# First MLP product by one Strassen step with seven half-k products in place of eight, interleaved with the second product

## The chip, the cores and the metric

The kernel runs on one core of one Trainium2 chip. The metric is the device time of one execution in microseconds (us), from the first to the last instruction with what the launch adds around them; lower is better. The engines are named as in the profile: PE is TensorE's matmul stream, PEld its weight loads, DVE is VectorE, ACT ScalarE, POOL GpSimd, and SP is SyncE, which issues nearly all DMAs, in order.

## The reference

One layer with two token groups (128 prompt tokens, 512 latent tokens; 640 rows together) and shared weights. The change touches the last line but two only:

```python
def layer(x, mod, p, lru_h0, gla_s0, rows):
    sh1, sc1, g1, sh2, sc2, g2 = jnp.split(mod, N_MOD, axis=-1)
    ng = p['norm_g']
    h = rmsnorm(x, ng[0]) * (1.0 + sc1) + sh1
    m, s_lru, s_gla = token_mix(h, p, lru_h0, gla_s0, rows)   # two recurrent mixers, w_out
    x = x + g1 * rmsnorm(m, ng[1])
    h = rmsnorm(x, ng[2]) * (1.0 + sc2) + sh2
    f = jnp.square(jax.nn.relu(h @ p['mlp_w1'])) @ p['mlp_w2']   # 640x1024 by 1024x4096, 640x4096 by 4096x1024
    x = x + g2 * rmsnorm(f, ng[3])
    return x, s_lru, s_gla
```

## The kernel before

Every fp32 product is made of three fp32r products: each operand x is split into a rounded part hi and a rest lo (ACT casts hi, DVE subtracts lo; `split_act` for activations, `split_piece` for weights), and PE adds hi*hi, hi*lo and lo*hi in PSUM.

The kernel records its whole program as a list of operations through `Recorder`, and `Recorder.order` then sets the order on each engine: a list scheduler with a cost for each operation, which gives out the buffers of each pool, respects data dependencies (`add` finds them by memory region), and prefers the operation recorded first (weight splits count as recorded 50 places earlier, `SPLIT_AHEAD`). Before the change, `region` treats a whole PSUM tile of two banks as one region. So a change of any dependency can move instructions anywhere in the program.

The MLP is cut into 16 groups g of 256 hidden columns (two blocks f of 128). In a group, `w1_units` makes hidden block f with features on partitions: 8 k-blocks by 3 terms by two halves of 320 rows, so 96 matmuls of 320 columns for the two blocks; `post_ff` takes relu (ACT), square (DVE), and the hi and lo parts `ah`, `al`. `w2_units` then multiplies with 256 rows of `mlp_w2`: 5 row tiles t by 2 blocks by 3 terms by 2 spans of 512 columns, 60 matmuls; `post_f` adds the result to the accumulators `fa`, `fb` in SBUF (DVE). In the main loop the units stand as w1 of group g, then w2 of group g-1. The first two groups (`NHALF` = 2) are made in two parts (rows 0 to 383, then the rest), because the rows of tiles 3 and 4 come later from the output projection (`out_pass`, `post_out`, `post_out_T`); `post_out_T` transposes the normed rows and writes the hi and lo parts H2H and H2L of the MLP's input. The last two groups of w2 share one pass with the final norm, gate and store (`post_f` with g = 15).

What the change leans on: the pool `tp` holds 43 tiles of 128 x 662 (`t_`), `wp` 4 split weight pieces (hi and lo each), `rawp` 2 raw weight loads of 1 MB, PSUM two `dense` and two `aux` tiles of two banks. The residual rows after the first half of the layer (`x1`, names xra and xrb in the trace) stay in ten tiles of `tp` until the end. A chain of DVE work that makes the gate rows g2 (`mod_chain`, names mw, mac) is fed in from group `G2_FROM` = 2 on. All operations are issued in one line of a helper, L340 in the profile, so groups are told apart by tile names.

```python
    for g in range(NHALF, NG):
        w1_units(g)
        if g == G2_FROM:
            units[-1].before = lambda: chains.extend(mod_g2)
        if g < NG - 1:
            w2_units([g - 1])
```

Of the kernel before, what the change touches and what calls it, by code (L numbers as in the profile page):

```python
# [8 lines left out]
F32 = mybir.dt.float32  # L9
F32R = mybir.dt.float32r  # L10
# [5 lines left out]
KT = 8  # L16
# [21 lines left out]
MH_ENG = "VAVV"  # L38
SPLIT_AHEAD = 50
POOL_OUT = (5,)  # L40
G2_FROM = 2
N_WARM = 24


# [65 lines left out]
class Recorder:  # L110
# [54 lines left out]
    @staticmethod  # L165
    def region(ap):

        return (0, 128, ((0, 1 << 30),)) if ap.space == bass.MemoryType.PSUM else _region(ap)

    def add(self, eng, name, args, kw):  # L170
        out = kw["out"] if "out" in kw else args[0]
        writes = [out] + ([kw["accum_out"]] if "accum_out" in kw else [])
        reads = [a for a in list(args if "out" in kw else args[1:]) + [v for k, v in kw.items() if k not in ("out", "accum_out")]
                 if hasattr(a, "ap")]
        if name == "copy_predicated" or (name == "matmul" and not kw["start"]):
            reads.append(out)
        o = Op()
        o.eng, o.name, o.args, o.kw, o.idx = eng, name, args, kw, len(self.ops)
        o.us = self.cost(eng, name, args, kw, out)
        o.rank = (o.idx - self.ahead, o.idx)  # L180
        o.users, o.tiles, o.ready, o.done, o.at = [], [], 0.0, None, None
        o.table = self.TABLE.get(args[2]) if name == "activation" else None
        deps = {}
        acc = [(a, True) for a in writes] + [(a, False) for a in reads]
        for a, w in acc:
            nm = getattr(a.tensor, "name", None)
            if a.space not in (bass.MemoryType.SB, bass.MemoryType.PSUM):
                continue
            r = self.region(a)
            if nm in self.tile_of and nm not in o.tiles:  # L190
                o.tiles.append(nm)
            h = self.hist.setdefault(nm, [])
            for q, qw, qr in h:
                both = a.space == bass.MemoryType.PSUM and q.eng != eng
                if (w or qw or both) and q is not o and _meet(r, qr):
                    deps[q.idx] = q
        for a, w in acc:
            if a.space not in (bass.MemoryType.SB, bass.MemoryType.PSUM):
# [144 lines left out]
class Piece:  # L343


    def __init__(self, load, view, rep=None):
        self.load, self.view, self.rep = load, view, rep
        self.hi = self.lo = None
        self.pool = False


# [37 lines left out]
def tile_hybrid_layer(  # L389
# [30 lines left out]
    def aux():  # L420
        return rec.tile(psa, 2, [128, 2, 512], F32, "aux", "a")
# [157 lines left out]
    def split_piece(p):  # L579
        hi = rec.tile(wp, N_W, [128, 1024], F32R, "whi", "whi")  # L580
        src = p.view(p.load.raw)
        lo = None
        if p.rep:
            hv = hi.rearrange("p (a r b) -> p a r b", a=KT, r=p.rep)
            for r in range(p.rep - 1):
                A.copy(hv[:, :, r, :], src)
            V.tensor_tensor(hv[:, :, p.rep - 1, :], src, f32(hv[:, :, 0, :]), op=OP.subtract)
        else:
            lo = rec.tile(wp, N_W, [128, 1024], F32R, "wlo", "wlo")
            hv = hi.rearrange("p (a b) -> p a b", a=src.shape[1])  # L590
            lv = lo.rearrange("p (a b) -> p a b", a=src.shape[1])
            A.copy(hv, src)
            (G if p.pool else V).tensor_tensor(lv, src, f32(hv), op=OP.subtract)
        p.hi, p.lo = hi, lo
        p.load.left -= 1
# [581 lines left out]
            after=lambda: prev is None or prev.done))  # L1177


    grow = {}  # L1180

    def mod_chain(part, nm, j, name):

# [41 lines left out]
        def fin_rows():  # L1225
            gi = 1 if nm == "g1" else 3
            br, gr = t_("br"), t_("gr")
            SP.dma_start(out=br[:, 0:512], in_=b_mod[0:1, col0:col0 + 512].to_broadcast([128, 512]))
            SP.dma_start(out=gr[:, 0:512], in_=norm_g[0, gi:gi + 1, 512 * j:512 * (j + 1)].to_broadcast([128, 512]))
            ps = aux()  # L1230
            for i in range(2):
                hi, lo = t_("mach", F32R), t_("macl", F32R)
                split_act(s["acc"][i][:, 0:512], hi[:, 0:512], lo[:, 0:512])
                for x in (hi, lo):
                    PE.matmul(ps[:, i, :], ones, x[:, 0:512], start=x is hi, stop=x is lo)
            for i in range(2):
                t = grow[nm, i, j] = t_(nm)
                V.tensor_tensor(t[:, 0:512], ps[:, i, :], br[:, 0:512], op=OP.add)
                V.tensor_tensor(t[:, 0:512], t[:, 0:512], gr[:, 0:512], op=OP.mult)

        fin = Stage(fin_rows if nm in ("g1", "g2") else fin_cols, 2.4 if nm in ("g1", "g2") else 0.4, gap=2)
        prev = mod_list[-1] if mod_list else None
# [124 lines left out]
        SP.dma_start(out=b[:, 0:512], in_=src[..., 512:1024])  # L1367
        xr[t] = (a, b)

    nrms = {}  # L1370

    def post_out(t, ps):
        i = 0 if t == 0 else 1
# [21 lines left out]
            nrm.append(n_)  # L1395
        nrms[t] = nrm

    def post_out_T(t):
        i, nrm = 0 if t == 0 else 1, nrms[t]
        ts = slice(128 * t, 128 * (t + 1))  # L1400
        for j in range(2):
            pst, hx = aux(), t_("hx")
            for k in range(4):
                PE.transpose(pst[:, 0, 128 * k:128 * (k + 1)], nrm[j][:, 128 * k:128 * (k + 1)], ident)
            for c0 in range(4):
                k = 4 * j + c0
                dst, src = hx[:, 128 * c0:128 * (c0 + 1)], pst[:, 0, 128 * c0:128 * (c0 + 1)]
                if j:
                    act(dst, src, AF.Identity, scale=cols["a2"][:, i, k:k + 1], bias=cols["sh2"][:, i, k:k + 1])
                else:  # L1410
                    V.tensor_scalar(dst, src, cols["a2"][:, i, k:k + 1], cols["sh2"][:, i, k:k + 1],
                                    op0=OP.mult, op1=OP.add)
            hv = hx[:, 0:512].rearrange("p (k c) -> p k c", k=4)
            split_act(hv, hbox["h"][:, 4 * j:4 * j + 4, ts], hbox["l"][:, 4 * j:4 * j + 4, ts])

    def out_pass(tiles, kinds):
        st = {}
# [3 lines left out]
        for u in range(4):  # L1421
            def run(t, u=u):
# [77 lines left out]
    NG = DFF // 256  # L1500

    HALVES, THIRDS = ((0, 512), (512, 1024)), ((0, 512), (512, 768), (768, 1024))

# [27 lines left out]

    def w2_units(gs):

        pcs = [row_pieces(mlp_w2, 2 * g) for g in gs]
        for t in range(NT):
            st = {}

# [7 lines left out]
            def run(n, t=t, st=st):  # L1545
# [3 lines left out]
                if n == 0:  # L1549
                    if last:  # L1550
                        st["ps"] = [p[:, 0, 0:c1 - c0] for p, (c0, c1) in zip((dense(), aux(), dense()), spans)]
                    else:
                        ps = dense() if t % 2 == 0 else aux()
                        st["ps"] = [ps[:, j, :] for j in range(2)]
                pss = st["ps"]
                if last:
# [10 lines left out]
                    post_f(t, pss, gs[-1], spans)  # L1567

            for n in range(len(gs)):
                units.append(Unit(pcs[n], [lambda n=n, run=run: run(n)], lambda: None, f"w2_{gs[n]}_{t}", us=2.6))  # L1570

    NHALF = 2
    n_mlp = len(units)
    for g in range(NHALF):
        w1_units(g, 0, 384, pair=g == 0)
# [3 lines left out]
    def before_rest():  # L1579
        for t in range(3, NT):  # L1580
            post_out_T(t)

    units[n_mlp + 2].before = before_rest
    for g in range(NHALF - 1):
        w2_units([g])
    for g in range(NHALF, NG):
        w1_units(g)
        if g == G2_FROM:
            units[-1].before = lambda: chains.extend(mod_g2)
        if g < NG - 1:  # L1590
            w2_units([g - 1])
    n_last = len(units)
    w2_units([NG - 2, NG - 1])
    units[n_last].before = lambda: flush(mod_g2)


    pieces, loads = [], []
# [83 lines left out]
```

## Time and profile before

| what | us |
|---|---|
| median of 3 runs | 1164.29 (1162.61 to 1165.95) |
| the profiled execution's own time | 1160.65 |
| its span (first to last instruction) | 1158.9 |
| PE busy in it | 1131.3 |
| PEld busy | 1064.3 |
| DVE busy | 755.6 |
| ACT busy | 557.8 |

The profile is of one execution. Busy time of an engine is the time in which it has an instruction in work; a wait is put down to the event that ended it. PE's rows give a start and a modelled length, and lengths of neighbours overlap, so the pace of matmuls is read from their starts.

### The profile page before, as it was taken

To read this page: it belongs to the slowest core of one execution; us is meant where nothing else is said; L and a number is where in the kernel's file an instruction comes from. 1 tells how busy PE (TensorE), PEld (TensorE's weight loads), DVE (VectorE), ACT (ScalarE), POOL (GpSimd) and SP (SyncE) were. 2 spreads that over 40 slices of the span, in tenths; PEclk is the share of its full clock that TensorE was granted. 3 is DMA by queue.
4 is the path that set the end of the run, shared out by engine and by line. 5 is a ranking of instruction groups with operands and counts; after the bars stand their busy time and mean duration, and the time that the engine had idled before them with its cause. 6 is when DMAs were issued, how large, how long until landed. Compare 5 with 4: busy or idle time off the path is not lost.

```text
span 1158.9 us, 17719 instructions
## 1 busy us (share of the span) xinstructions
PE 1131.3 (98%) x7188; PEld 1064.3 (92%) x7188; DVE 755.6 (65%) x1147; ACT 557.8 (48%) x882; POOL 80.1 (7%) x152
## 2 busy tenths in 40 slices
PE   6999999999999999999999999999999999999996
PEld 5899899999999999999999879999999989999995
DVE  4687885966557557549968389885444555555546
ACT  6387989994657668213432388422222222222222
POOL 3135112000000000000000021000000000000001
PEclk9999999999999999999999999999999999999999
DMA  9835445332121312245535356532222222222202
GB/s 296 253 78 142 132 110 132 93 104 77 52 92 40 102 60 83 64 158 207 191 128 182 112 179 199 192 118 74 73 73 74 73 73 73 78 81 86 85 1 90
DMA packets 101009, 130.63 MB, mean 113 GB/s; under 512 B 7790, under 2 KB 77632, under 8 KB 100928
## 3 DMA queue, kind: packets, MB, share of 16 engines
q1 hardware_dynamic: 98880, 127.61, 35.6%
q0 software_dynamic: 2048, 1.90, 0.7%
q8 instruction: 56, 0.92, 0.3%
q14 instruction: 25, 0.20, 0.1%
HBM read 117.94 MB, written 3.68 MB: 105 GB/s over the span
## 4 chain that ended last, share of the span: by engine, by line
PE 78%; DVE 8%; ACT 5%; DMA 5%; issue 2%; POOL 1%; SPq 0%; DVEq 0%; POOLq 0%; ACTq 0%
PE dense L340 62%; PE aux L340 16%; DVE i L340 2%; DVE th L340 2%; DMA i<-r 1%; DVE wlo L340 1%; DMA modw<-in_w_mod_dram 1%; ACT L340 1%; ACT r L340 1%; ACT th L340 1%; DMA raw<-in_w_in_dram 1%; DMA w2raw<-in_gla_w_dram 1%; DMA r<-r 1%; ACT whi L340 1%; ACT L339 0%
## 5 line engine op out<-in xcount | busy, mean ns | idle before, releaser
L340 ACT CAST whi<-raw 128x1024 fp32r<-128x1024 f32 (+1 forms) x159 | 164.5, 1038 | 394.2 <-PE dense L340 363.6
L340 DVE TENSOR_TENSOR wlo<-raw,whi 128x1024 fp32r<-128x1024 f32 x154 | 188.1, 1223 | 173.5 <-ACT whi L340 173.1
L340 PE MATMUL dense<-HH,whi 128*128 128x320 f32 x768 | 178.1, 312 | 0.2 <-ACT vc L340 0.2
L340 PE MATMUL dense<-HL,whi 128*128 128x320 f32 x768 | 176.1, 310 | 0.0
L340 PE MATMUL dense<-HH,wlo 128*128 128x320 f32 x752 | 172.4, 309 | 0.0
L340 PEld LDWEIGHTS dense<-HH,whi 128*128 128x128 f32 x768 | 128.4, 188 | 2.1 <-issue 0.8
L340 PEld LDWEIGHTS dense<-HL,whi 128*128 128x128 f32 x768 | 128.9, 188 | 0.0
L340 PEld LDWEIGHTS dense<-HH,wlo 128*128 128x128 f32 x752 | 125.9, 188 | 0.0
L340 PE MATMUL dense<-H2H,whi 128*128 128x320 f32 (+2 forms) x496 | 116.8, 309 | 0.0
L340 PE MATMUL dense<-H2H,wlo 128*128 128x320 f32 (+2 forms) x496 | 116.4, 308 | 0.0
L340 PE MATMUL dense<-H2L,whi 128*128 128x320 f32 (+2 forms) x496 | 116.4, 308 | 0.0
L340 PEld LDWEIGHTS dense<-H2H,whi 128*128 128x128 f32 x496 | 84.5, 188 | 1.3
L340 PEld LDWEIGHTS dense<-H2L,whi 128*128 128x128 f32 x496 | 84.0, 188 | 0.0
L340 PEld LDWEIGHTS dense<-H2H,wlo 128*128 128x128 f32 x496 | 84.0, 188 | 0.0
L340 DVE SCALAR_TENSOR_TENSOR mac<-mw,cst,mac 128x512 f32<-128x512 f32 x112 | 77.9, 747 | 2.9 <-DMA mw<-in_w_mod_dram 2.7
L340 PE MATMUL dense<-wlo,ah 128*128 128x512 f32 (+1 forms) x192 | 75.3, 392 | 0.0
L340 PE MATMUL dense<-whi,ah 128*128 128x512 f32 (+1 forms) x192 | 75.3, 392 | 0.0
L340 PE MATMUL dense<-whi,al 128*128 128x512 f32 (+1 forms) x192 | 75.3, 392 | 0.0
L340 PE MATMUL aux<-wlo,ah 128*128 128x512 f32 (+1 forms) x132 | 51.7, 392 | 0.0
L340 PE MATMUL aux<-whi,ah 128*128 128x512 f32 (+1 forms) x132 | 51.7, 391 | 0.0
L340 PE MATMUL aux<-whi,al 128*128 128x512 f32 (+1 forms) x132 | 51.6, 391 | 0.0
L340 PE MATMUL dense<-whi,HH 128*128 128x256 f32 x160 | 45.0, 281 | 0.0
(311 smaller groups left out, 2172.6 us busy)
## 6 DMA issues: line engine op xcount, KB each, us to landing
raw<-in_mlp_w_dram SPq DMA_DIRECT2D x34, 1024.0 KB, 5.7
raw<-in_w_in_dram SPq DMA_DIRECT2D x24, 1024.0 KB, 5.5
mw<-in_w_mod_dram SPq DMA_DIRECT2D x64, 256.0 KB, 5.6
modw<-in_w_mod_dram SPq DMA_DIRECT2D x32, 256.0 KB, 6.1
raw<-in_w_out_dram SPq DMA_DIRECT2D x8, 1024.0 KB, 4.9
i<-r SPq DMA_DIRECT2D x32, 160.0 KB, 2.6
raw<-in_w_in_dram SPq DMA_DIRECT2D x8, 512.0 KB, 4.0
raw<-in_lru_up_dram SPq DMA_DIRECT2D x4, 1024.0 KB, 5.1
```

The costliest lines, as they stand in the source:

```text
L340: getattr(eng[o.eng], o.name)(*o.args, **o.kw)
```

## The change

For groups 2 to 15 the first product is made from a 2 by 2 by 2 split: the 1024 input features are cut into halves of 4 k-blocks, the 640 rows into halves L and R of 320, and the 256 hidden columns of the group are the two blocks. Seven products of half-k (4 k-blocks by 3 terms, 12 matmuls of 320 columns) replace eight. The sums of the inputs are made once (`make_forms`: tiles f42, f42l, f3, and H2H/H2L columns R of features 0 to 511 overwritten), the sums of the weights for each group (`make1` to `make4`, tiles s1, s2, in halves of a weight piece), and the partial results are combined by accumulation in three PSUM banks X, Y, Z of `aux` tiles with copies of the state in between taken by ACT (`sq`) and DVE (`sq`, `z1`, `z2`). The square moves from DVE to ACT (`post`). The four w1 units of a group alternate with the five w2 units of the group before; all w2 tiles of the middle groups use `dense` banks.

Around it: `region` now knows PSUM by bank; `post_out_T` keeps the transposed input in fp32 (hx0 to hx7) and `split_h` splits it in two calls; `post_out` stores the residual rows in DRAM, and `before_last` loads them again ahead of the last two groups of w2; the gate rows g2 go to DRAM and back too; `G2_FROM` is 6.

```diff
-G2_FROM = 2
+G2_FROM = 6
...
-        return (0, 128, ((0, 1 << 30),)) if ap.space == bass.MemoryType.PSUM else _region(ap)
+        if ap.space == bass.MemoryType.PSUM:
+            runs = _region(ap)[2]
+            return (0, 128, ((runs[0][0] // 512 * 512, -(-runs[-1][1] // 512) * 512),))
+        return _region(ap) if ap.space == bass.MemoryType.SB else (0, 128, ((0, 1 << 30),))
...
+        xd[t] = rec.tile(dr, 1, [128, 1024], F32, f"xd{t}", f"xd{t}")
+        for j in range(2):
+            SP.dma_start(out=xd[t][:, 512 * j:512 * (j + 1)], in_=x1[t][j][:, 0:512])
...
-            hv = hx[:, 0:512].rearrange("p (k c) -> p k c", k=4)
-            split_act(hv, hbox["h"][:, 4 * j:4 * j + 4, ts], hbox["l"][:, 4 * j:4 * j + 4, ts])
+
+    def split_h(c0, c1):
+        for k in range(KT):
+            split_act(h32[k][:, c0:c1], hbox["h"][:, k, c0:c1], hbox["l"][:, k, c0:c1])
...
+                    if t == 2:
+                        split_h(0, 384)
...
+    def make_forms(k):
...
+        u, l = h32[k], h32[k + 4]
+        V.tensor_tensor(u[:, L_], u[:, L_], u[:, R_], op=OP.subtract)
+        V.tensor_tensor(u[:, R_], l[:, R_], u[:, R_], op=OP.subtract)
+        V.tensor_tensor(l[:, R_], l[:, R_], u[:, L_], op=OP.add)
+        V.tensor_tensor(l[:, L_], l[:, L_], l[:, R_], op=OP.subtract)
+        split_act(l[:, 0:T], f42[k][:, 0:T], f42l[k][:, 0:T])
+        split_act(u[:, L_], hbox["h"][:, k, R_], hbox["l"][:, k, R_])
+        c = slice(320 * (k % 2), 320 * (k % 2 + 1))
+        split_act(u[:, R_], *(f3[k // 2 * 2 + n][:, c] for n in range(2)))
...
+        def make1(r, hi, lo):
+            s1, s2 = s["s1"], s["s2"] = kv(t_("s1")), kv(t_("s2"))
+            split_act(blk(r, 0, 0), kv(hi), kv(lo))
+            V.tensor_tensor(s1, blk(r, 1, 0), blk(r, 1, 1), op=OP.add)
+            V.tensor_tensor(s2, s1, blk(r, 0, 0), op=OP.subtract)
+            split_act(s2, kv(hi, 1), kv(lo, 1))
...
+        def post(f, z, parts):
+            ah, al = ffs[f] = (t_("ah", F32R), t_("al", F32R))
+            for c in parts:
+                act(z[:, c], z[:, c], AF.Relu)
+            act(z[:, 0:T], z[:, 0:T], AF.Square)
+            split_act(z[:, 0:T], ah[:, 0:T], al[:, 0:T])
...
+        def p1():
+            ps = aux()
+            s["X"], s["Y"], s["q"] = ps[:, 0, L_], ps[:, 1, L_], t_("sq")
+            product(s["X"], 0, 0, "B11", True, False)
+            A.copy(s["q"][:, L_], s["X"])
+
+        def p6():
+            product(s["Y"], 1, 0, "T2", True, False)
+            V.tensor_tensor(s["q"][:, R_], s["q"][:, L_], s["Y"], op=OP.add)
+
+        def p5():
+            s["Z"] = aux()[:, 0, L_]
+            product(s["Z"], 0, 1, "T1", True, False)
+
+        def p7():
+            z = s["z2"] = t_("z2")
+            product(s["Y"], 1, 1, "T3", False, False)
+            V.tensor_tensor(z[:, R_], s["q"][:, L_], s["Y"], op=OP.add)
+            V.tensor_tensor(z[:, R_], z[:, R_], s["Z"], op=OP.subtract)
+
+        def p2():
+            z = s["z1"] = t_("z1")
+            product(s["X"], 0, 2, "B21", False, True)
+            act(z[:, L_], s["X"], AF.Relu)
+
+        def p4():
+            z = s["z2"]
+            product(s["Y"], 1, 2, "T4", False, True)
+            V.tensor_tensor(z[:, L_], s["q"][:, L_], s["Y"], op=OP.add)
+            post(2 * g + 1, z, (slice(0, T),))
+
+        def p3():
+            z = s["z1"]
+            product(s["Z"], 0, 3, "B22", False, True)
+            V.tensor_tensor(z[:, R_], s["q"][:, R_], s["Z"], op=OP.subtract)
+            post(2 * g, z, (R_,))
...
+    for k in range(4):
+        units[n_forms + k].before = lambda k=k: make_forms(k)
     for g in range(NHALF, NG):
-        w1_units(g)
+        a_ = fast_units(g)
...
+        b_ = w2_units([g - 1]) if g < NG - 1 else []
+        for n in range(max(len(a_), len(b_))):
+            units.extend(a_[n:n + 1] + b_[n:n + 1])
...
+        for t in range(NT):
+            x1[t] = (t_("xra"), t_("xrb"))
+            for j in range(2):
+                SP.dma_start(out=x1[t][j][:, 0:512], in_=xd[t][:, 512 * j:512 * (j + 1)])
```

The order that the scheduler makes of it, at three places. First DVE in a middle group, before the change: from the last two adds of one w2 pass over the first product of the next group (wlo are weight splits, rl and al the square and the rest of a hidden block, fa and fb the accumulators).

```order
L340 TENSOR_TENSOR wlo<-raw,whi 128x1024
L340 TENSOR_TENSOR fa<-fa,dense 128x512
L340 TENSOR_TENSOR fb<-fb,dense 128x512
L340 TENSOR_TENSOR wlo<-raw,whi 128x1024 x2
L340 TENSOR_TENSOR rl<-rl 128x640
L340 TENSOR_TENSOR al<-rl,ah 128x640
L340 TENSOR_TENSOR wlo<-raw,whi 128x1024
L340 TENSOR_TENSOR rl<-rl 128x640
```

And DVE in a middle group of the change, from the last fb of one w2 pass over products 6 and 7 of the next group (s are sums of weight blocks, sq and z the partial results).

```order
L346 TENSOR_TENSOR fb<-fb,dense 128x512
L346 TENSOR_TENSOR sq<-sq,aux 128x320
L346 TENSOR_TENSOR wlo<-raw,whi 128x1024
L346 TENSOR_TENSOR fa<-fa,dense 128x512
L346 TENSOR_TENSOR fb<-fb,dense 128x512
L346 TENSOR_TENSOR s_1262<-raw 128x512
L346 TENSOR_TENSOR s_1263<-s_1262,raw 128x512
L346 TENSOR_TENSOR raw<-raw 128x4x128
L346 TENSOR_TENSOR z_1251<-sq,aux 128x320
L346 TENSOR_TENSOR wlo<-s_1233,whi 128x512
L346 TENSOR_TENSOR z_1251<-z_1251,aux 128x320
```

Reads of partial sums (sq, z) now stand between the adds of the second product and the weight sums, one piece of work of DVE after the other.

Second, DVE at the step from the first two groups to group 2: before, with the first w2 pass (fb copies) stood the g2 chain (mac).

```order
L340 COPY fb_1152<-aux_1150 128x512
L340 SCALAR_TENSOR_TENSOR mac_1170<-mw_1180,cst32_113,mac_1170 128x512
L340 SCALAR_TENSOR_TENSOR mac_1171<-mw_1180,cst32_113,mac_1171 128x512
L340 SCALAR_TENSOR_TENSOR mac_1170<-mw_1181,cst32_113,mac_1170 128x512
L340 COPY fb_1155<-dense_1153 128x512
```

In the change the sums of the inputs stand there (hx; f42l and H2L are their rests; whi_1182 and whi_1185 are the next weight pieces, which take the buffers of the two pieces of this w2 pass).

```order
L346 COPY fb_1171<-dense_1169 128x512
L346 TENSOR_TENSOR hx3_1034<-hx3_1034 128x320
L346 TENSOR_TENSOR wlo_1183<-raw_1145,whi_1182 128x1024
L346 TENSOR_TENSOR f42l_1166<-hx6_1037,f42_1165 128x640
L346 TENSOR_TENSOR hx3_1034<-hx7_1038,hx3_1034 128x320
L346 TENSOR_TENSOR wlo_1186<-s1_1148,whi_1185 128x512
L346 TENSOR_TENSOR hx7_1038<-hx7_1038,hx3_1034 128x320
L346 TENSOR_TENSOR raw_1136<-raw_1136 128x4x128
L346 TENSOR_TENSOR hx7_1038<-hx7_1038 128x320
L346 TENSOR_TENSOR H2L_1024<-hx3_1034,H2H_1023 128x320
L346 TENSOR_TENSOR wlo_1186<-raw_1136,whi_1185 128x512
L346 TENSOR_TENSOR f3_1168<-hx3_1034,f3_1167 128x320
```

The next row there is f42l_1173, the last input sum's rest, and then fb_1176<-aux_1174; the first is read by the last three matmuls of group 2's product 6, the second frees the bank of its product 5.

Third, SP near the end of the change, where xd and gd are the rows kept in DRAM and raw the last load of w2's weights.

```order
L346 DMA raw<-in_mlp_w_dram 128x2x1024
L346 DMA g_1632<-gd_1389 128x512
L346 DMA g_1633<-gd_1496 128x512
L346 DMA g_1634<-gd_1391 128x512
L346 DMA g_1635<-gd_1498 128x512
L346 DMA xra<-xd_1030 128x512
L346 DMA xrb<-xd_1030 128x512
L346 DMA xra<-xd_1051 128x512
L346 DMA xrb<-xd_1051 128x512
L346 DMA xra<-xd_1059 128x512
L346 DMA xrb<-xd_1059 128x512
L346 DMA raw<-in_mlp_w_dram 128x2x1024
```

Ten reloads have come in ahead of the last weight load, which before followed the load ahead of it at once.

## Rows read from the trace of the kernel before

**Rows 1.** The page: span, then busy time, share and instructions of engines.

```profile
span 1158.9 us, 17719 instructions
...
PE 1131.3 (98%) x7188; PEld 1064.3 (92%) x7188; DVE 755.6 (65%) x1147; ACT 557.8 (48%) x882; POOL 80.1 (7%) x152
```

**Rows 2.** Windows of stretches: length, busy time of PE, PEld, DVE, ACT, POOL, clock.

```profile
core 0: us, PE busy (x) PEld busy (x) DVE busy (x) ACT busy (x) POOL busy (x), PEclk, DMA share, GB/s
...
100.00:200.00 100.00, 97.11 (x699) 96.23 (x698) 72.26 (x100) 93.39 (x114) 18.69 (x32) 1.00 0.45 122
200.00:300.00 100.00, 97.42 (x699) 95.91 (x698) 74.24 (x114) 74.00 (x104) 1.21 (x1) 1.00 0.33 94
...
660.00:700.00 40.00, 38.24 (x179) 30.82 (x178) 32.31 (x57) 30.65 (x56) 8.20 (x8) 1.00 0.52 155
700.00:740.00 40.00, 40.00 (x251) 37.51 (x250) 37.93 (x67) 25.08 (x51) 2.74 (x3) 1.00 0.72 234
740.00:1120.00 380.00, 380.00 (x2127) 344.47 (x2126) 209.22 (x271) 96.17 (x114) 0.00 (x0) 1.00 0.24 77
...
1150.00:1159.00 9.00, 0.00 (x0) 0.00 (x0) 3.59 (x8) 1.00 (x4) 1.44 (x2) 0.70 0.39 117
```

**Rows 3.** Timeline of PE, one group: start, length, instruction.

```profile
799.50 0.46 PE L340 MATMUL dense<-H2H,whi 128*128 128x320 f32 x2
...
813.59 0.39 PE L340 MATMUL dense<-whi,ah 128*128 128x512 f32 x1
...
827.50 0.45 PE L340 MATMUL dense<-H2H,whi 128*128 128x320 f32 x2
```

**Rows 4.** Timeline of PE, 256-column matmuls, three apart.

```profile
719.73 0.28 PE L340 MATMUL dense<-H2H,wlo 128*128 128x256 f32 x1
...
720.08 0.28 PE L340 MATMUL dense<-H2H,wlo 128*128 128x256 f32 x1
```

**Rows 5.** Groups by shape, 700 to 1130 us: busy, mean ns, idle before.

```profile
L340 PEld LDWEIGHTS dense<-H2H,whi 128*128 128x128 f32 x496 | 84.5, 188 | 1.3
...
L340 DVE TENSOR_TENSOR wlo<-raw,whi 128x1024 fp32r<-128x1024 f32 x66 | 80.7, 1224 | 114.8 <-ACT whi L340 114.6
...
L340 ACT CAST whi<-raw 128x1024 fp32r<-128x1024 f32 x64 | 67.3, 1051 | 244.9 <-PE dense L340 238.4 <-issue 4.6 <-DMA raw<-in_mlp_w_dram 1.8
...
L340 DVE TENSOR_TENSOR fa<-fa,dense 128x512 f32<-128x512 f32 x40 | 27.4, 685 | 19.7 <-PE dense L340 19.7
...
L340 DVE TENSOR_TENSOR al<-rl,ah 128x640 fp32r<-128x640 f32 x28 | 23.0, 822 | 11.3 <-ACT ah L340 11.3
...
L340 ACT CAST ah<-rl 128x640 fp32r<-128x640 f32 x28 | 20.4, 728 | 39.4 <-DVE rl L340 39.4
L340 DVE SCALAR_TENSOR_TENSOR mac<-mw,cst,mac 128x512 f32<-128x512 f32 x28 | 20.3, 747 | 2.9 <-DMA mw<-in_w_mod_dram 2.7
...
L340 DVE TENSOR_TENSOR rl<-rl 128x384 f32<-128x384 f32 x4 | 2.1, 552 | 0.0
...
L340 DVE TENSOR_TENSOR rl<-rl 128x256 f32<-128x256 f32 x4 | 1.7, 424 | 0.6 <-ACT rl L340 0.6
```

**Rows 6.** Timeline: last matmul into a bank, and the add that reads it.

```profile
787.19 0.39 PE L340 MATMUL dense<-whi,al 128*128 128x512 f32 x1
...
787.62 0.69 DVE L340 TENSOR_TENSOR fa<-fa,dense 128x512 f32<-128x512 f32 x1
```

**Rows 7.** Timeline: DVE in the first w2 pass; PE at its end.

```profile
734.65 2.07 DVE L340 SCALAR_TENSOR_TENSOR mac<-mw,cst,mac 128x512 f32<-128x512 f32 x3
...
741.57 0.46 PE L340 MATMUL dense<-H2H,whi 128*128 128x320 f32 x2
```

**Rows 8.** DMA issues: count, KB of one, median us from issue to landing.

```profile
raw<-in_mlp_w_dram SPq DMA_DIRECT2D x34, 1024.0 KB, 5.7
...
mw<-in_w_mod_dram SPq DMA_DIRECT2D x64, 256.0 KB, 5.6
```

More of the change, by code (lines that the diff above doesn't have):

```diff
@@ L186, in add @@
             nm = getattr(a.tensor, "name", None)
-            if a.space not in (bass.MemoryType.SB, bass.MemoryType.PSUM):
+            if not self.tracked(a):
                 continue
@@ L197, in add @@
         for a, w in acc:
-            if a.space not in (bass.MemoryType.SB, bass.MemoryType.PSUM):
+            if not self.tracked(a):
                 continue
@@ L582, in split_piece @@
         lo = None
-        if p.rep:
+        if p.make:
+            lo = rec.tile(wp, N_W, [128, 1024], F32R, "wlo", "wlo")
+            p.make(src, hi, lo)
+        elif p.rep:
             hv = hi.rearrange("p (a r b) -> p a r b", a=KT, r=p.rep)
@@ L1239, in fin_rows @@
                 V.tensor_tensor(t[:, 0:512], t[:, 0:512], gr[:, 0:512], op=OP.mult)
+                if nm == "g2":
+                    gd[nm, i, j] = rec.tile(dr, 1, [1, 512], F32, f"gd{i}{j}", f"gd{i}{j}")
+                    SP.dma_start(out=gd[nm, i, j], in_=t[0:1, 0:512])
         fin = Stage(fin_rows if nm in ("g1", "g2") else fin_cols, 2.4 if nm in ("g1", "g2") else 0.4, gap=2)
@@ L1368, in load_x @@
         xr[t] = (a, b)
-    nrms = {}
+    nrms, xd, h32 = {}, [None] * NT, []
     def post_out(t, ps):
@@ L1400, in post_out_T @@
         ts = slice(128 * t, 128 * (t + 1))
+        if t == 0:
+            h32.extend(t_(f"hx{k}") for k in range(KT))
         for j in range(2):
-            pst, hx = aux(), t_("hx")
+            pst = aux()
             for k in range(4):
@@ L1498, in w1_units @@
                     c0=c0, c1=c1, tag=f"w1_{f}", psum=(lambda f=f: bank(f)) if pair else None)
-    NG = DFF // 256
+    NG, NHALF = DFF // 256, 2
+    L_, R_ = slice(0, 320), slice(320, T)
+    form = {}
+    f42, f42l, f3 = [], [], []
+    def make_forms(k):
+        for lst, nm, n in ((f42, "f42", 1), (f42l, "f42l", 1), (f3, "f3", 2 * (1 - k % 2))):
+            lst.extend(t_(nm, F32R) for _ in range(n))
+        u, l = h32[k], h32[k + 4]
[7 more added lines that the diff above has]
+        split_act(u[:, R_], *(f3[k // 2 * 2 + n][:, c] for n in range(2)))
+        if k < 3:
+            return
+        H, L = hbox["h"], hbox["l"]
+        form["B11"] = lambda k: (H[:, k, L_], L[:, k, L_])
+        form["B21"] = lambda k: (H[:, 4 + k, L_], L[:, 4 + k, L_])
+        form["B22"] = lambda k: (H[:, 4 + k, R_], L[:, 4 + k, R_])
+        form["T1"] = lambda k: (H[:, k, R_], L[:, k, R_])
+        form["T2"] = lambda k: (f42[k][:, R_], f42l[k][:, R_])
+        form["T4"] = lambda k: (f42[k][:, L_], f42l[k][:, L_])
+        form["T3"] = lambda k: tuple(f3[k // 2 * 2 + n][:, 320 * (k % 2):320 * (k % 2 + 1)] for n in range(2))
@@ new lines, in fast_units, with make2, make3, make4 @@
+    def fast_units(g):
+        ld = Load(w1_r[:, :, 256 * g:256 * (g + 1)], [128, 8, 256], 4)
+        s = {}
+        blk = lambda r, i, j: r[:, 4 * j:4 * (j + 1), 128 * i:128 * (i + 1)]
+        kv = lambda t, n=0: t[:, 512 * n:512 * (n + 1)].rearrange("p (k m) -> p k m", k=4)
+        def make1(r, hi, lo):
[4 more added lines that the diff above has]
+            split_act(s2, kv(hi, 1), kv(lo, 1))
+        def make2(r, hi, lo):
+            split_act(s["s1"], kv(hi), kv(lo))
+            s3 = blk(r, 1, 0)
+            V.tensor_tensor(s3, blk(r, 0, 0), s3, op=OP.subtract)
+            split_act(s3, kv(hi, 1), kv(lo, 1))
+        def make3(r, hi, lo):
+            for t, w in ((hi, None), (lo, hi)):
+                v = t.rearrange("p (k m) -> p k m", k=4)
+                if w is None:
+                    A.copy(v, r[:, 4:8, :])
+                else:
+                    V.tensor_tensor(v, r[:, 4:8, :], f32(w.rearrange("p (k m) -> p k m", k=4)), op=OP.subtract)
+        def make4(r, hi, lo):
+            V.tensor_tensor(s["s2"], s["s2"], blk(r, 0, 1), op=OP.subtract)
+            split_act(s["s2"], kv(hi), kv(lo))
+        pcs = []
+        for m in (make1, make2, make3, make4):
+            p = Piece(ld, lambda r: r)
+            p.make = m
+            pcs.append(p)
+        def product(ps, n, w, x, first, last):
+            p = pcs[w]
+            for k in range(4):
+                if w == 2:
+                    hi, lo = (t[:, 256 * k + 128 * n:256 * k + 128 * (n + 1)] for t in (p.hi, p.lo))
+                else:
+                    hi, lo = (kv(t, n)[:, k, :] for t in (p.hi, p.lo))
+                xh, xl = form[x](k)
+                for m, (ww, xx) in enumerate(((hi, xh), (hi, xl), (lo, xh))):
+                    PE.matmul(ps, ww, xx, start=first and k == 0 and m == 0,
+                              stop=k == 3 and m == 2, skip_group_check=not first)
+        def post(f, z, parts):
[34 more added lines that the diff above has]
+            post(2 * g, z, (R_,))
+        return [Unit([p], fs, lambda: None, f"w1_{g}_{n}", us=1.76 * len(fs), dve=d, act=a_)
+                for n, (p, fs, d, a_) in enumerate(zip(pcs, ((p1, p6), (p5, p7), (p2, p4), (p3,)),
+                                                       (1.7, 1.6, 1.1, 1.8), (0.5, 0.1, 2.4, 1.7)))]
@@ L1532, in w2_units @@
     def w2_units(gs):
-        pcs = [row_pieces(mlp_w2, 2 * g) for g in gs]
+        pcs, us = [row_pieces(mlp_w2, 2 * g) for g in gs], []
         for t in range(NT):
@@ L1569, in w2_units @@
             for n in range(len(gs)):
-                units.append(Unit(pcs[n], [lambda n=n, run=run: run(n)], lambda: None, f"w2_{gs[n]}_{t}", us=2.6))
-    NHALF = 2
+                us.append(Unit(pcs[n], [lambda n=n, run=run: run(n)], lambda: None, f"w2_{gs[n]}_{t}", us=2.6))
+        return us
     n_mlp = len(units)
```

29 lines of the change are left out of this document (19 added, 10 removed).

## The prediction

> **What bounds the kernel now.** I read the page first: PE is busy for 1131.3 of 1158.9 us, DVE for 755.6, ACT for 557.8 [rows 1]. That a matmul stream is always busy would not prove that it is the bound, so the windows come next. From 740 to 1120 us, the 14 groups that the change rewrites, PE is busy for 380.00 of 380 us at clock 1.00, while DVE works 209.22 and ACT 96.17 [rows 2]: nothing is ever waited for there. PE's 27.6 us of idle time lie elsewhere: 2.9 and 2.6 us in 100 to 300 us, 1.8 us in 660 to 700, 9.0 us after the last matmul [rows 2], the rest at the start. Then the pace, from starts: a group's 96 matmuls of 320 columns take 813.59 - 799.50 = 14.09 us, 0.1468 us each, its 60 of 512 columns 827.50 - 813.59 = 13.91 us, 0.232 each [rows 3]; a group takes 28.0 us. In the stretch to be changed, fewer columns are fewer microseconds as long as DVE and ACT keep up.
>
> **What the change removes.** Each of 14 groups loses 12 of its 96 matmuls of 320 columns: 12 x 0.1468 = 1.76 us, 24.7 us in all. A group becomes 84 x 0.1468 + 13.91 = 26.2 us. Every product still has 320 columns, so the pace should hold.
>
> By the Trainium skill (TensorE: Matmul & The Clock Gate, Back-to-back issue gap) a warm matmul takes its columns at 2.4 GHz plus 2.5 ns, so 0.1358 us here; the gain would be an estimated 22.8 us by that page. The rows say 0.1468 and decide; the gain by them is 24.7.
>
> **What it adds to DVE and ACT.** DVE in a middle group: ten accumulator adds (0.685), three rests of 1024 columns (1.224), five rests and four weight sums of 512 (nine at 0.685), five reads of partial sums of 320, two rests of 640 (0.822) [rows 5]. No row has 320 columns; the nearest are 0.424 (256) and 0.552 (384), I take 0.49. Sum: 6.85 + 3.67 + 6.17 + 2.45 + 1.64 = 20.8 us of 26.2, 79%; before it was 6.85 + 4 x 1.224 + 4 x 0.822 = 15.0 of 28.0. ACT gets three casts of 1024 (1.051), five of 512 and three reads of 320 (each at most the 0.728 of 640 columns), and five passes of 640 (0.728): at most 12.6 us of 26.2. Both fit, so the cost is nothing where each result is in time; PE's own 26.2 us are the cover, and DVE has 5.4 us of it left in a group.
>
> In time means the seven products. Product 7 adds into bank Y, which DVE must have read after product 6; product 4 again into Y after 7; 2 into X after 1; 3 into Z after 5. Between each pair PE has other work: a w2 unit (12 x 0.232 = 2.78 us) and one product (1.76) at the least, 4.5 us, in groups 2 to 14. The hand-over costs the start of the read, about 0.2 us (the matmul that starts at 787.19 streams for 0.23, the add starts at 787.62 [rows 6]), the read, 0.49, and the way back, which I set at 0.2 too: 0.9 us, and in the order DVE has at most a rest of 1024 or two adds of 512 ahead (1.2 to 1.4 us). 2.3 against 4.5: hidden. Group 15 has no w2 pass beside it; there the least cover is one product, 1.76 us, against 0.9.
>
> **The step into the first group.** The sums of the inputs are four rounds of about 3.8 us of DVE (six operations of 320 columns at 0.49, one rest of 640; the cast goes to ACT). They stand where the g2 chain's mac operations stood, three in a row for 2.07 us between two copies [rows 7], and DVE was full before that too: 37.93 of 40 us from 700 to 740 [rows 2]. So DVE is late here, and the order shows for what. The rests wlo_1183 and wlo_1186 wait for the buffers of the first w2 pass, whose last six matmuls end about 741.57 [rows 7] and begin 1.39 us earlier, at 740.2. After the latter ACT needs 0.2 + 1.05 us, so DVE starts wlo_1183 about 741.6. From there to f42l_1173 there are eleven operations in the order: 1.22 + 0.82 + 0.82 (two of 640), five of 320 (0.49) and three of 512 (0.685), 7.4 us by mean lengths; but neighbours overlap by about 0.08 us (three mac operations of 0.747 take 2.07 [rows 5, 7]), which takes it to 6.5: ready at 748.1. PE meanwhile has product 1 (1.76), nine matmuls of product 6 (1.32) and a w2 unit (2.78) and stands at 747.4. It waits 0.7 to 1.6 us for the last three, and 0.2 us more for the bank of product 5. I take 1.0; the ends are 0, if DVE comes early, and 3, if its backlog of the whole stretch (15 us of sums in some 20 us, where the 20 us of mac were spread over 40) shows.
>
> **Smaller terms.** Splitting the transposed input in two calls (eight rests of 384 at 0.552, 4.4 us in one piece, ahead of weight rests of w_out): between 0 and 1.5 us; 0.5 taken, since PE already waited 1.8 us in that stretch. The mac chain of g2, 20.3 us of DVE [rows 5], moves into the groups from 6 on, by the order over five of them: 4.1 us a group where 5.4 are left. DVE is nearly full there: 0 to 2 us, 0.5 taken. Stores of the residual rows: ten DMAs of 256 KB on SP among loads that have whole groups of time, nothing waits for them. At the end, ten reloads (2.5 MB) stand on SP ahead of the last w2 weights (1 MB). At the best rate of these windows, 234 GB/s, the ten need 11.2 us, and the load 5.7 more [rows 2, 8]; its pieces are needed 12.3 us (group 15's products) + 4.4 us (19 matmuls of w2) after its buffer is free, less a cast and a rest (2.3): 14.4. So 0 to 2.5 us; 0.5 taken, since several reloads can start earlier. The tail after the last matmul, 9.0 us, keeps its work.
>
> **Sum.** -24.7 + 1.0 + 0.5 + 0.5 + 0.5 = -22.2 us, against this execution's own 1160.65 (span 1158.9): 1138.5. The median of the runs shown stands 3.6 us above it, so 1142 us is forecast for the median.
>
> **The rivals.**
>
> *The program ahead of the MLP moves.* `region` by banks changes dependencies in every PSUM tile, and the order differs from the first products on. PE idles 27.6 us in all, 9.0 in the tail and 1.8 near 690, so at most 16.8 us can be won; ACT is busy for 93.39 of 100 us from 100 on [rows 2], and the order has one table load more there. For: that stretch is full. Against: PE waits only 5.5 us in 200 us, so most shifts fall in slack. I give 3 us either way: 1139 where it wins, 1145 where it loses.
>
> *DVE and SP hold PE up at both ends.* All upper bounds of the steps above at once: 3 + 1.5 + 2 + 2.5 = 9 in place of 2.5: 1149.
>
> *Hand-overs of partial sums (the other side).* If DVE comes to each read late, PE stands before every product that adds into a bank just read: 4 x 14 = 56 places. The gain is gone at 24.7 / 56 = 0.44 us each; with the whole hand-over of 0.9 us exposed the time is 1164.3 - 24.7 + 50 = 1190. For: DVE goes from 54 to 79% and works in order. Against: 4.5 us of cover for 2.3.
>
> *Weight loads set the pace.* Every matmul has a load of 0.188 us beside it [rows 5]. Until now two of six brought new weights, the others the same again; in the change two of three do. If the pace fell to that of the loads, 84 x 0.188 = 15.8 us would stand where 14.09 stood: 1164 + 14 x 1.7 = 1188 us. It decides at 14.09 / 84 = 0.168 us a matmul. Against: the 256-column matmuls bring new weights in two of three too, with loads of the same length, and come every (720.08 - 719.73) / 3 = 0.117 us [rows 4], so loads run beside each other and beside matmuls. The Trainium skill (Perfetto Trace Analysis, Identifying the Most-Contended Engine) would judge PE by the share of its weight loads, here 92% [rows 1], and not by its matmuls'. That share doesn't bind here, by those rows.
>
> *The change does not do what it says.* Fewer columns that don't shorten the stretch at all: 1164. Nothing in rows 2 and 3 speaks for it.
>
> **How the numbers follow.** Chances: forecast (1140 to 1144) 0.50; early part wins 0.13, loses 0.11; both ends held up 0.17; hand-overs 0.04; weight loads 0.02; no effect 0.03. The range takes in the first four, 1136 to 1151: from the forecast less 3 us of early gain and the two smaller terms at 0, up to 1149 with a little early loss. About 0.3% (3.5 us) is what a measurement of this kernel can tell from no change; faster by more than that 0.91 (the first four cases), within it 0.03, slower 0.06.
>
> **What would show it.** Right: in the middle groups PE still without idle time, 26.2 us from one group's product 1 to the next, matmuls of 320 columns 0.147 apart; DVE near 75% of that stretch by its windows and ACT near 40%; PE waits of 1 us or so in total for f42l or an fb copy at the first rewritten group; PE idle before 660 us within 3 us of before. Wrong: waits of PE on sq or z in every group (hand-overs), starts 0.168 us or more apart (weight loads), or a wait for w2's last weights near the end.

## The result and the profile after

The changed kernel takes 1215.30 us (median of 4 runs, 1214.93 to 1217.86) where the kernel before takes 1163.51 beside it: a ratio of 1.0446, 95% interval [1.0424, 1.0469]. It is 52 us slower; 22 us faster was forecast. Its profiled execution has a span of 1213.2 us.

The page after (compare [rows 1]):

```profile
span 1213.2 us, 17825 instructions
...
PE 1131.8 (93%) x7020; PEld 1036.6 (85%) x7020; DVE 840.8 (69%) x1335; ACT 622.4 (51%) x1013; POOL 81.0 (7%) x152
```

PE issues 168 matmuls fewer, as meant, and DVE works 85 us more. PE's busy time is a poor witness: the last matmul ahead of a stop counts as busy for 0.40 us and the first behind it for 0.50 (lines below), where an undisturbed one takes 0.232 from start to start, so busy time stays level while the span grows. Starts and counts tell more. The windows after (compare [rows 2]):

```profile
200.00:300.00 100.00, 95.11 (x680) 92.95 (x679) 75.53 (x112) 76.43 (x106) 0.00 (x0) 1.00 0.34 95
...
700.00:740.00 40.00, 38.72 (x248) 36.43 (x246) 36.69 (x71) 31.94 (x68) 3.26 (x4) 1.00 0.58 180
740.00:1120.00 380.00, 341.07 (x1775) 288.59 (x1774) 274.18 (x425) 140.26 (x212) 0.00 (x0) 1.00 0.26 83
```

In the stretch that had no idle time at all, PE now starts 1775 matmuls where it started 2127, at clock 1.00 as before: it stands still. DVE is busy 72% there, so no engine is full. What PE waits for in the MLP, from the view of waits, 740 to 1204 us (total us, times, longest):

```profile
PE dense L346 <- DVE fa L346: 28.1, 36, 0.8
PE aux L346 <- ACT z L346: 7.4, 14, 0.5
PE aux L346 <- ACT sq L346: 6.8, 13, 0.6
PE dense L346 <- ACT fa L346: 1.3, 2, 0.7
```

The first row is the surprise. `fa` is the accumulator of the *second* product, whose units the change only moved. Before, PE never waited for it. The timeline of the changed kernel shows one such place:

```profile
787.56 0.40 PE L346 MATMUL dense<-whi,ah 128*128 128x512 f32 x1
788.00 0.69 DVE L346 TENSOR_TENSOR fa<-fa,dense 128x512 f32<-128x512 f32 x1 [1.59 <-PE dense L346]
...
788.74 0.50 PE L346 MATMUL dense<-wlo,ah 128*128 128x512 f32 x1 [0.78 <-DVE fa L346]
...
789.08 0.39 PE L346 MATMUL dense<-whi,al 128*128 128x512 f32 x1
...
789.31 0.31 PE L346 MATMUL aux<-H2H,whi 128*128 128x320 f32 x1
```

These are the last three matmuls of one w2 unit, all into the second bank of its tile. The first bank is complete three matmuls earlier, and DVE's add of it (fa) begins at 788.00. The next matmul, into the *other* bank, starts only when that add is done. In [rows 6] the same add begins after the unit's last matmul, beside the next unit's first. The built order of the changed kernel shows why (the bracket is a wait on DVE's semaphore, put there at build time; numbers name tiles):

```
3312 L346 MATMUL dense_1239<-whi_1212,ah_1197 128x512
3313 L346 MATMUL dense_1239<-wlo_1213,ah_1197 128x512 [waits DVE_49]
3314 L346 MATMUL dense_1239<-whi_1212,al_1198 128x512
```

Since `region` knows PSUM by bank, the scheduler may place a read of bank 0 among the matmuls into bank 1. But the framework below it guards the *tile*: it sees a read of dense_1239 and then a write to dense_1239, and makes the write wait. Price of a stop, from starts: 789.08 - 787.56 = 1.52 us for what takes 2 x 0.232, so 1.05 us; the 0.78 that the view of waits shows is only the idle part.

The partial sums do the same, since X and Y share a tile. Product 6 (into Y) is stopped by ACT's copy of X:

```profile
791.22 0.31 PE L346 MATMUL aux<-f42l,whi 128*128 128x320 f32 x1
...
791.56 0.43 ACT L346 COPY sq<-aux 128x320 f32<-128x320 f32 x1 [0.91 <-PE aux L346]
792.04 0.19 PEld L346 LDWEIGHTS aux<-f,wlo 128*128 128x128 f32 x1 [0.78 <-ACT sq L346]
792.04 0.41 PE L346 MATMUL aux<-f,wlo 128*128 128x320 f32 x1 [0.52 <-ACT sq L346]
...
792.29 0.31 PE L346 MATMUL aux<-f,whi 128*128 128x320 f32 x1
```

That costs 1.07 - 2 x 0.147 = 0.78 us. By these prices the 36 stops on fa make 37.8 us and the 27 on sq and z 21.1.

By the Trainium skill (PSUM — Partial Sum Buffer, Summary: rules for kernel authors) PSUM read while a matmul runs should be in a different bank, guarded by bank. The order obeys that rule; the guard it runs under is coarser. Whether the chip itself lets the two go side by side is what run `e5_dense_one_bank` shows.

### The profile page after: what moved, and what is told of

The parts are those of the page before. It is cut to its first block, busy times and chain, and to the rows that moved or that the text cites. A ratio compares the mean times of both kernels' runs of the same rounds, so it can differ in the third digit from the quotient of the medians.

```text
span 1213.2 us, 17825 instructions
## 1 busy us (share of the span) xinstructions
PE 1131.8 (93%) x7020; PEld 1036.6 (85%) x7020; DVE 840.8 (69%) x1335; ACT 622.4 (51%) x1013; POOL 81.0 (7%) x152
## 4 chain that ended last, share of the span: by engine, by line
PE 76%; ACT 8%; DVE 7%; issue 3%; POOL 2%; DMA 2%; SPq 0%; DVEq 0%; ACTq 0%; POOLq 0%
PE dense L346 52%; PE aux L346 24%; DVE fa L346 2%; DMA i<-r 2%; ACT junk L346 1%; DVE i L346 1%; POOL spp L346 1%; ACT whi L346 1%; ACT r L346 1%; DVE wlo L346 1%; ACT L346 1%; ACT th L346 1%; ACT L345 1%; ACT z L346 1%; POOL bdr L346 0%
## 5 line engine op out<-in xcount | busy, mean ns | idle before, releaser
L346 ACT CAST whi<-raw 128x1024 fp32r<-128x1024 f32 (+2 forms) x173 | 167.0, 969 | 251.0 <-PE dense L346 164.1
L346 DVE TENSOR_TENSOR wlo<-raw,whi 128x1024 fp32r<-128x1024 f32 (+1 forms) x168 | 190.0, 1133 | 69.9 <-ACT whi L346 68.4
L346 PEld LDWEIGHTS dense<-whi,al 128*128 128x128 f32 x288 | 54.0, 188 | 33.8 <-DVE fa L346 21.9
L346 PEld LDWEIGHTS dense<-wlo,ah 128*128 128x128 f32 x288 | 54.0, 188 | 32.2 <-DVE fa L346 21.9
L346 PE MATMUL aux<-H2H,wlo 128*128 128x320 f32 (+1 forms) x240 | 75.1, 313 | 1.9 <-DVE z L346 1.2
L346 PE MATMUL aux<-H2H,whi 128*128 128x320 f32 (+1 forms) x240 | 74.7, 311 | 0.0
L346 PE MATMUL aux<-H2L,whi 128*128 128x320 f32 (+1 forms) x240 | 74.7, 311 | 0.0
L346 DVE TENSOR_TENSOR fa<-fa,dense 128x512 f32<-128x512 f32 x66 | 45.3, 686 | 32.2 <-PE dense L346 31.8
L346 PE MATMUL aux<-f,wlo 128*128 128x320 f32 x168 | 54.7, 326 | 13.6 <-ACT z L346 6.9
L346 PEld LDWEIGHTS dense<-whi,ah 128*128 128x128 f32 x288 | 54.1, 188 | 9.9
L346 PE MATMUL aux<-f,whi 128*128 128x320 f32 x224 | 59.4, 309 | 0.0
```

Source lines behind the costliest of these rows:

```text
L346: getattr(eng[o.eng], o.name)(*o.args, **o.kw)
```

## The experiments

**Theory A**: the loss comes from order by bank under a guard by tile, and neither from Strassen nor from DVE's load. **Theory B**: DVE is late with the partial sums of the seven products (the rival with hand-overs). **Theory C**: the other parts cost it. All runs compute the full result; each is compared with the kernel before on its own chip.

**The region rule alone, in the kernel before.**

```diff
-        return (0, 128, ((0, 1 << 30),)) if ap.space == bass.MemoryType.PSUM else _region(ap)
+        if ap.space == bass.MemoryType.PSUM:
+            runs = _region(ap)[2]
+            return (0, 128, ((runs[0][0] // 512 * 512, -(-runs[-1][1] // 512) * 512),))
+        return _region(ap)
```

> The kernel before with one part of the change alone: region knows PSUM by bank. No Strassen product, no rows in DRAM. Theory A (guard by tile): the order now puts an add of fa, which reads the first bank of a tile, ahead of the last matmuls into the second bank, and the matmul after it waits because the tile as a whole is guarded. The built order has 53 more such waits inside w2 tiles than before; at 0.78 us each that is 41 us in the MLP, plus about 8 us ahead of it: 1200 to 1215 us, with PE waits on DVE fa. Theory B (DVE is late with the partial sums of the seven products): there are none here, so the time stays at that of before, 1160 to 1167. Theory C (the rest of the change costs it: order of units, rows in DRAM, g2 chain later): also 1160 to 1167.

1234.78 us, ratio 1.0617 [1.0590, 1.0645]: slower than the changed kernel itself, with no Strassen product in it. Waits of PE, 740 to 1220 us, and one place in its timeline:

```profile
PE dense L343 <- DVE fa L343: 20.3, 26, 0.8
PE aux L343 <- DVE fa L343: 20.3, 26, 0.8
```

```profile
1105.46 0.40 PE L343 MATMUL dense<-whi,ah 128*128 128x512 f32 x1
1105.90 0.69 DVE L343 TENSOR_TENSOR fa<-fa,dense 128x512 f32<-128x512 f32 x1 [1.64 <-PE dense L343]
1106.64 0.50 PE L343 MATMUL dense<-wlo,ah 128*128 128x512 f32 x1 [0.78 <-DVE fa L343]
1106.97 0.39 PE L343 MATMUL dense<-whi,al 128*128 128x512 f32 x1
```

What B and C blame is not in this kernel, and still it loses 71.6 us; whether either adds to the loss of the changed kernel is left to the next runs. 52 stops were counted, 53 expected. My size was low by 20 us or more: I had priced a stop at its idle time (0.78, not 1.05), and the loss ahead of the MLP at 8 us where group 2 starts 20.3 us later (761.85 against 741.57). From there to the last matmul it needs 462.48 us in place of 408.13: 54.35 us for 52 stops, 1.05 each.

**The change without the region rule** (a whole tile is one region again), and **the same with X and Z in one tile, Y alone**, the first edit and then the second on top:

```diff
-        if ap.space == bass.MemoryType.PSUM:
-            runs = _region(ap)[2]
-            return (0, 128, ((runs[0][0] // 512 * 512, -(-runs[-1][1] // 512) * 512),))
...
-            s["X"], s["Y"], s["q"] = ps[:, 0, L_], ps[:, 1, L_], t_("sq")
+            s["X"], s["Z"], s["q"] = ps[:, 0, L_], ps[:, 1, L_], t_("sq")
...
         def p6():
+            s["Y"] = aux()[:, 0, L_]
...
-            s["Z"] = aux()[:, 0, L_]
```

> The changed kernel with region knowing PSUM by whole tile again, as before; everything else of the change stays. Theory A: the waits of w2 matmuls on fa go (43.7 us of them between 730 and 1190), those of products on sq and z go in part, since X and Y share a tile and the order can only put other matmuls between them: 1140 to 1160. Theory B: DVE has the same work, the waits come back under other names, 1205 to 1220. Theory C: 1205 to 1220 as well.

> As the run with region by whole tile, and X and Z now share one tile of two banks while Y has one to itself; with that, a read of a partial sum is followed in the order by a w2 unit or another product before its tile is written again. Theory A: PE runs through the groups with hardly a wait, 26.2 us a group, 1136 to 1146, the time that was forecast for the change. Theory B: DVE is still late, waits on sq and z of about 1 us a group or more stay, over 1165. Theory C: over 1165.

1140.39 us, 0.9804 [0.9780, 0.9828], and 1138.06 us, 0.9789 [0.9767, 0.9811]: both as A expects, and not to be told from each other. Both beat the kernel before and the changed kernel. Windows and waits (741 to 1128 us) of the second:

```profile
200.00:300.00 100.00, 97.43 (x701) 96.02 (x700) 74.29 (x112) 74.84 (x105) 1.21 (x1) 1.00 0.34 94
...
740.00:1120.00 380.00, 378.65 (x2064) 338.87 (x2063) 305.90 (x472) 161.69 (x245) 1.56 (x3) 1.00 0.32 102
```

```profile
PE dense L343 <- DVE fb L343: 0.7, 1, 0.7
PE aux L343 <- DVE fb L343: 0.7, 1, 0.7
```

DVE is busier than in the changed kernel (305.90 of 380 us against 274.18), since the same work fits in less time, and yet PE waits twice in 14 groups. That disposes of B.

**By bank for aux tiles only**, which takes the stops on fa away and keeps those on sq and z:

```diff
-    @staticmethod
-    def region(ap):
+    def region(self, ap):
...
-        if ap.space == bass.MemoryType.PSUM:
+        if ap.space == bass.MemoryType.PSUM and self.tile_of.get(ap.tensor.name) != "d":
```

> The changed kernel with region by whole tile for dense tiles and by bank for aux tiles only. Theory A: the waits on fa go (43.7 us of idle weight loads in the MLP, 28.1 us by the matmul rows), those on sq and z (some 21 us) and part of the waits ahead of the MLP stay: 1168 to 1188. Theories B and C: within 5 us of the changed kernel, 1210 to 1220.

1171.65 us, 1.0074 [1.0051, 1.0097]: as expected. Taken back in this order, dense tiles by bank cost 43.7 us (1215.3 - 1171.65), aux tiles by bank 31.3 (1171.65 - 1140.39).

**Order by bank, guard by bank**: each dense tile becomes two tiles of one bank (`Two` makes them as they are first used), `region` stays as in the change.

```diff
-    psd = ctx.enter_context(tc.tile_pool(name="psd", bufs=2, space=bass.MemoryType.PSUM))
+    psd = ctx.enter_context(tc.tile_pool(name="psd", bufs=4, space=bass.MemoryType.PSUM))
...
-        return rec.tile(psd, 2, [128, 2, 512], F32, "dense", "d")
+        return Two(lambda: rec.tile(psd, 4, [128, 512], F32, "dense", "d"))
```

> The changed kernel with its order by bank kept, and each dense tile of two banks made as two tiles of one bank, so that the guard covers what the order assumes; aux tiles stay as they are. (Reads across both banks of a dense tile in the program ahead of the MLP become two instructions.) Theory A (guard by tile): an add of fa that stands ahead of the last matmuls of its unit no longer stops them; the PE waits on fa in w2 units go though fa is read just as early, and the time comes near that of the run with dense by whole tile, 1165 to 1185, the waits on sq and z of aux staying. Rival (the early read itself costs, by a collision of DVE's read and PE's write in PSUM, or by DVE's order): PE still stops or slows there, 1205 to 1220.

1179.13 us, 1.0134 [1.0116, 1.0153]. Its timeline at the end of a w2 unit:

```profile
1048.22 0.39 PE L389 MATMUL dense<-whi,ah 128*128 128x512 f32 x1
...
1048.42 0.69 DVE L389 TENSOR_TENSOR fa<-fa,dense 128x512 f32<-128x512 f32 x1
1048.45 0.40 PE L389 MATMUL dense<-wlo,ah 128*128 128x512 f32 x1
...
1048.68 0.40 PE L389 MATMUL dense<-whi,al 128*128 128x512 f32 x1
...
1048.92 0.31 PE L389 MATMUL aux<-H2H,whi 128*128 128x320 f32 x1
```

This is the key run: fa reads its bank at least as early as in the changed kernel, in the same place of the unit, and PE writes the bank beside it at an unbroken 0.23 us. The early read costs nothing here; the guard does. Two waits on DVE's fa are left in the MLP, both in aux tiles, which are still guarded as a whole. (By the Trainium skill, PSUM — Partial Sum Buffer, same section, this is the form to use, and the trace agrees.)

**Order by bank, but no room for the read**: the spans of w2 alternate matmul by matmul, so the first bank is complete only one matmul before the end.

```diff
                     for i in range(2):
-                        for ps, span in zip(pss, spans):
-                            mm(ps, n, i, span, ts)
+                        for m in range(3):
+                            for ps, span in zip(pss, spans):
+                                mm(ps, n, i, span, ts, m)
```

> The changed kernel, region by bank kept, with one edit in the loop of w2: the two spans alternate from matmul to matmul, where they alternated every three, so the first bank is complete one matmul (0.23 us) ahead of the last of the second, not three. Theory A: the order has no room to put fa ahead of the unit's last matmul, the waits on fa go, those on sq and z stay: 1165 to 1185. Rival (the early read itself, or DVE's load): 1205 to 1220.

1173.38 us, 1.0082 [1.0063, 1.0101]. Its waits from 730 us on start with these two; none on fa is left:

```profile
PE aux L346 <- ACT z L346: 7.4, 14, 0.5
PE aux L346 <- ACT sq L346: 6.8, 13, 0.6
```

Three ways of taking the stops on fa away (order, guard, loop) end within 8 us of one another. Of the 7.5 us between the first two, 5.3 stand ahead of group 2, which starts at 753.22 in the run with dense by whole tile and at 758.55 in the one with one-bank tiles.

**The alternating loop on the good version, and the g2 chain at group 2 again**, each by itself on the version with X and Z paired; the first is the diff just shown, the second

```diff
-G2_FROM = 6
+G2_FROM = 2
```

> The run with X and Z in one tile and region by whole tile, with the alternating loop of w2 on top: a pair of matmuls into two banks now shares its weights. Theory A: nothing is left to gain from it, since PE hardly waits any more and its matmuls are paced by their columns: 1135 to 1141, the same as without it. If weight loads had a part in the pace of 0.232 us, the 512-column matmuls would come closer together and the time fall by more than 3 us.

> The run with X and Z in one tile and region by whole tile, with the g2 chain started at group 2 as before the change. My reading: DVE has room in the groups, so where the 20 us of the chain stand matters little: 1136 to 1142. If DVE is near its limit at the step into the first rewritten groups, the chain there costs 2 to 6 us more: 1140 to 1144.

1141.38 us, 0.9800 [0.9780, 0.9819], and 1138.92 us, 0.9791 [0.9770, 0.9811], against 0.9789 without either edit: no difference that can be told, though the first median lies 0.4 us above the range expected. The alternating loop puts matmuls with the same weights side by side, but the weights are still loaded for each (2061 loads from 740 to 1120 us, 2063 without it), so what fewer loads would do is not shown.

**The change without Strassen and without the region rule.**

```diff
-        a_ = fast_units(g)
+        w1_units(g)
+        a_ = []
...
-                        ps = dense() if t % 2 == 0 or NHALF <= gs[0] < NG - 2 else aux()
+                        ps = dense() if t % 2 == 0 else aux()
```

> The change without its Strassen step and with region by whole tile: groups 2 to 15 make the first product in eight half-k products as before (w1_units), the input and weight sums are not made, and w2 takes dense and aux tiles in turn as before. What stays of the change: residual and gate rows kept in DRAM and reloaded, the input split in two calls, the g2 chain from group 6. Theory A: these cost next to nothing by themselves, 1161 to 1167, so all that the whole-tile versions gain comes from the 168 matmuls left out. Theory C (they cost several us, hidden in the sum): over 1168, and the Strassen step would be worth more than 24.7 us.

1163.26 us, 0.9997 [0.9985, 1.0009]. C falls: rows in DRAM, the split in two calls and the later chain together cost nothing that can be measured.

The PE timelines of these kernels, read for starts:

| kernel | first product of group 2 starts | a group takes | last matmul starts |
|---|---|---|---|
| before | 741.57 | 28.03 (799.50 to 1107.85, 11 groups) | 1149.70 |
| changed | 758.34 | 32.02 (1066.40 to 1098.42) | 1204.08 |
| before, region by bank | 761.85 | 32.19 (1082.69 to 1114.88) | 1224.33 |
| changed, dense in one-bank tiles | 758.55 | 27.82 (1043.73 to 1071.55) | 1167.89 |
| changed, whole tile, X and Z paired | 741.95 | 26.29 (1036.31 to 1062.60) | 1127.01 |
| no Strassen, whole tile | 743.89 | 28.01 (743.89 to 771.90) | 1151.51 |

A steady group of the changed kernel (1066.40 to 1098.42) has four stops on fa, at 1072.29, 1079.39, 1092.33 and 1095.95, and two on sq and z, at 1067.22 and 1082.71: 4 x 1.05 + 2 x 0.78 = 5.8 us, and 26.29 + 5.8 = 32.1. With region by bank alone it has four on fa: 28.03 + 4.2 = 32.2. With one-bank dense tiles two are left: 26.29 + 1.56 = 27.85. All three meet the table. Not every group of the changed kernel is like this one: some have fewer stops, and from the stop in product 6 of group 2 (761.07) to that of group 15 (1163.27) a group takes 30.9 us on average.

## Why the prediction was wrong

**The step that failed** is the rival "the program ahead of the MLP moves". It saw that region by banks "changes dependencies in every PSUM tile", and then costed only what a different order could do, 3 us either way, in the early program. It did not ask what enforces an order once it is built: a wait per tile, whatever the scheduler believes. In place of 3 us the runs show 71.6 for this one edit alone in the kernel before (1234.78 against 1163.16), and 75 in the changed kernel (1215.30 against 1140.39), some 60 of these from group 2 on. With that the sentence on middle groups, PE "still without idle time, 26.2 us", went too. The step was missing for the stretch that mattered most and for units (w2) whose cost I had left alone. The order rows that I quoted were DVE's; PE's order with its waits would have shown the stop.

Against the version with X and Z paired, the changed kernel starts group 2 by 16.4 us later and needs 445.74 us from there to its last matmul in place of 385.06, 60.7 more. From group 2 on the stops make 37.8 + 21.1, three more (one on fa in an aux tile, two on DVE's z) and one wait on wlo about 3.2: 62.1 us, less the 1.6 that the paired version loses at its own two waits, 60.5 for 60.7 measured. Ahead of group 2 new waits of the same kind appear: four on ACT's fa between 740 and 758 us, 0.95 each from starts (744.17 - 742.76 less 2 x 0.232), and these, the largest from 60 to 740 us of the changed kernel:

```profile
PE dense L346 <- ACT va L346: 4.3, 4, 2.2
PE aux L346 <- ACT junk L346: 3.7, 6, 0.6
PE aux L346 <- DVE u L346: 2.8, 5, 0.6
```

va is the copy of the first bank of a tile whose second is being filled. That whole-tile regions give the 16.4 us back is shown: group 2 starts at 753.22 with dense tiles alone by whole tile, at 743.74 with aux tiles too, at 741.95 with X and Z paired besides. How they divide among the single waits was not separated. With dense tiles of one bank group 2 still starts at 758.55: the waits on va are gone, but PE waits once for 4.2 us on DVE's la. So the key run shows the guard as the cause in the w2 units; ahead of group 2 the order by bank may also cost by itself, which no run separates.

**The other steps**, measured where the stops are gone:

- *12 matmuls a group at 0.1468 us, 24.7 in all*: right. A group goes from 28.03 to 26.29 or 26.24 (1062.60 to 1088.84), 1.76 us on average, and with all else at nothing by the run without Strassen, 0.9997 to 0.9789 is 24 us.
- *DVE at 79%*: 305.90 of 380 is 80%; the read of 320 columns that I put at 0.49 takes 0.484 in the changed kernel:

```profile
L346 DVE TENSOR_TENSOR z<-sq,aux 128x320 f32<-128x320 f32 x42 | 20.3, 484 | 44.9 <-PE aux L346 44.8
```

- *First rewritten group, 1.0, and the moved g2 chain, 0.5*: right in kind. PE waits twice on copies or adds of fb, at 749.08 and 927.47; measured from starts this costs 0.82 and 0.77 us. The first is product 6 waiting for its tile, which a copy of fb frees; where X and Z are not paired PE waits for f42l there, as forecast, 0.4 us (at 750.26). The second goes with the chain: with the chain at group 2 it stands at 823.03, the first at 749.71. *Input split, 0.5*: product 1 of group 2 starts 0.4 us later, which was not separated from the rest of that stretch. *Reloads at the end, 0.5*: no wait, 0. Sum of the small terms 2.0 for 2.5.
- *Hand-overs of partial sums*: wrong as a rival, as its cover argument said. Where the stops are gone, DVE and ACT are in time for all 56; the stop comes inside a tile, not between products that add into one bank. Its price (50 us) and its sign (waits on sq or z in every group) were near what happened, so that the sign alone would have named the wrong cause.
- *Weight loads set the pace*: wrong. Matmuls of 320 columns come every 0.147 us in the changed kernel too (789.31 to 791.07, 12 of them).

So the sum, 1142 us (1136 to 1151), holds for the change without the region edit: 1140.39 us, or 1138.06 with X and Z paired. The kernel as written carries that edit too, and it costs 75 us where the Strassen step brings 24.

## What to carry to other kernels

When a scheduler's idea of a dependency is made finer, check that the guard below it is as fine: either both go by bank (tiles of one bank) or neither. A row in which PE waits for a reader of the tile it is still filling is the sign; its price is the gap between starts, not the idle time shown. And of a change in several parts, cost the one-line helper first, since it touches every tile.

## What the runs showed of the hardware

DVE's read of one PSUM bank (0.69 us for 128x512) does not slow PE's writes to the next bank: 0.23 us a matmul through it (1048.22 to 1048.92). A stop of 0.78 us idle costs 1.05: the matmul ahead of it counts as busy for 0.40 us where it would have taken 0.232 from start to start, and the two starts after the stop are 0.34 us apart in place of 0.232. The granted clock stayed 1.00 with four such stops in 32 us. And with DVE at 80% of the stretch, working in order, PE met two waits of 0.7 us in 14 groups with 56 hand-overs of partial sums.
